# Rotating rope queries from one product instead of two, in a two-layer hybrid backbone on one core

## The chip, the cores and the metric

The kernel runs on 1 core of a Trainium2 chip. The metric is device time of one execution in microseconds (us), as the median of three runs. Within the core, TensorE does matmuls, VectorE and ScalarE read their results from PSUM and write SBUF, GpSimd (POOL in the rows) works on SBUF, and SyncE (SP) issues most of the transfers. Each engine runs its own instructions in order and waits for the others by semaphores.

## The reference, cut to what matters

The reference is a diffusion backbone of two layers over 1024 latent tokens of width 1024, with 256 context tokens. The even layer runs gated linear attention (GLA) and multi-head latent attention (MLA) side by side; the odd layer mixes by Fourier transforms and chunked gating. The change touches one thing, the rope part of the MLA queries. A low-rank latent of 256 is normalised and multiplied by `w_uq`, which gives each of 8 heads 64 plain features and 32 rope features; the rope features are then rotated by an angle for each token, their two halves of 16 acting as the two coordinates:

```python
def apply_rope(x, cos, sin):
    xf = x.astype(jnp.float32)
    x1, x2 = jnp.split(xf, 2, axis=-1)
    return jnp.concatenate([x1 * cos - x2 * sin, x1 * sin + x2 * cos], -1).astype(x.dtype)

q = jnp.einsum('bnr,re->bne', rms_norm(cq, q_norm_g), w_uq).reshape(B, n, MLA_HEADS, MLA_NOPE + MLA_ROPE)
q_nope, q_rope = q[..., :MLA_NOPE], q[..., MLA_NOPE:]
q_rope = apply_rope(q_rope, rope[0][:, None, :], rope[1][:, None, :])
s = (einsum('bqhd,bkhd->bhqk', q_nope, k_nope) + einsum('bqhr,bkr->bhqk', q_rope, k_rope)) * MLA_SCALE
```

Scores, softmax and the product with the values follow for each head over all 1280 keys.

## The kernel before, in words

Everything is held transposed: features on the 128 partitions, tokens along the free dimension in halves of 512. Products are made in three passes (`mm3`, lines 144 to 148): each fp32 operand is split into a high part, rounded to fp32r by ScalarE, and a low part, the difference, by VectorE (`split`, line 131); a product is then high by high, low by high and high by low, accumulated in one PSUM bank. So a contraction over 256 features is six matmuls for 128 output rows and 512 tokens.

The work is written as Python generators that yield an estimate of their cost. `weave` (line 51) advances the stream that has used the smallest share of its weight; the order that results is the program's order, which the framework's own planner then takes as priorities when it lays out each engine's queue. Waits are placed by the framework.

The rope queries are made in `mla_qr` (line 929), four heads at a time: 4 x 32 features are 128 output rows. It is called twice. The first call, for heads 0 to 3, is in `mla_ramp` (line 868). This is the prologue of the attention; it is woven (line 1507) with the last input projections, `in_proj_b`, whose gate tiles need a weight from DRAM, a ScalarE cast and a SiLU. The second call, for heads 4 to 7, is put ahead of the preparation of head 4 and woven with `attend(3)` (lines 1096 to 1104).

A call does for each half of the tokens: load a cosine and a sine table of 128x512 through SP; multiply the latent by the rope columns (one product) and by the same columns with the two halves of each head swapped (a second product, from another 256 columns of the weight); multiply the first by the cosine table, the second by the sine table, whose first 16 rows of each head hold the sine with its sign turned (two VectorE instructions that read PSUM, lines 945 and 946); add them (line 947); and split the sum into `qr`. The weight `k.wq[1]` holds both sets, 512 columns, and is loaded and split at the start of the ramp.

`mla_prep` (line 973) makes one head's operands. Score matmuls contract over 97 partitions: 64 plain features, 32 rope features and one row for the running maximum. These rows have to lie together, so SP moves them from SBUF to SBUF (`move`, line 179): 64 rows of keys (`kt`), 64 plain query rows from `qn` and 32 rope rows from `qr`, each for the high and the low part. All moves are issued by SP in order. Then 24 matmuls `psm` of the high parts give scores for the row maximum, which VectorE reduces; they are the first to use a head's moved rows. `attend` follows, with score matmuls `pss`, exponentials and splits by ScalarE, VectorE and GpSimd, and the value matmuls `psav`. While head h is attended, head h + 1 is prepared.

Of the kernel before, what the change touches and what calls it, by code (L numbers as in the profile page):

```python
# [867 lines left out]
def mla_ramp(k):  # L868

    nc, A = k.nc, k.A  # L870
    k.wq = []
    for i in range(2):
        k.wq.append(k.weight(A["wuq"][i], (P, 2, 512)))
        yield 0.5
    k.cqn = []
    for t in range(2):
        x = k.b4(name="cq")
        nc.sync.dma_start(x, k.cqd[t])
        k.cqn.append(k.split(x, (P, N)))
        yield 0.5  # L880
    x, xc = k.b4(name="ckvr"), k.w2((P, L), name="ckvx")
    nc.sync.dma_start(x, k.ckvd[:, 0:N])
    nc.sync.dma_start(xc, k.ckvd[:, N:])
    cx = k.b4(F32R, (P, 2, L), name="ckx")
    k.ckn = [(a, cx[:, i, :]) for i, a in enumerate(k.split(x, (P, N)))]
    k.split(xc, None, hi=cx[:, 0, :], lo=cx[:, 1, :])
    yield 1.0
    k.wkv = k.weight(A["wukv"], (P, 1024))
    yield 1.0

    k.ktx = k.b4(F32R, (P, 4, L), name="ktx")
    k.kt = [None, None]
    k.Q, k.R = [None] * 8, {}
    yield from mla_qr(k, 0)
    mla_keys(k, 0)
    yield 1.0
    yield from mla_qk(k, 0)
    yield from mla_prep(k, 0)
    assert k.mg_done
    for t in range(4):  # L900
        x = k.b4(name="mg")
        nc.sync.dma_start(x, k.mgd[t])
        k.act(x, x, AF.Silu)
        nc.scalar.dma_start(k.mgd[t], x)
        yield 0.5
# [23 lines left out]
def mla_qr(k, hd):  # L929

    nc, A = k.nc, k.A
    qr = k.R["qr"] = (k.b4(F32R, name="qrh"), k.b4(F32R, name="qrl"))
    for s in range(0, N, 512):
        o = slice(s, s + 512)
        cos, sin = k.w2(name="cos"), k.w2(name="sin")
        nc.sync.dma_start(cos, A["cos"][:, o])
        nc.sync.dma_start(sin, A["sin"][:, o])
        pp = []
        for sw in range(2):
            ps = k.bank()  # L940
            c0 = 256 * sw + 32 * hd
            for kk in range(2):
                k.mm3(ps, (k.wq[1][0][:, kk, c0:c0 + P], k.wq[1][1][:, kk, c0:c0 + P]), (k.cqn[kk][0][:, o], k.cqn[kk][1][:, o]), kk == 0, kk == 1)
            pp.append(ps)
        nc.vector.tensor_tensor(out=cos, in0=pp[0], in1=cos, op=ALU.mult)
        nc.vector.tensor_tensor(out=sin, in0=pp[1], in1=sin, op=ALU.mult)
        nc.vector.tensor_tensor(out=cos, in0=cos, in1=sin, op=ALU.add)
        k.split(cos, None, hi=qr[0][:, o], lo=qr[1][:, o])
        yield 2.6


def mla_qk(k, hd):
# [20 lines left out]
def mla_prep(k, hd):  # L973

    nc = k.nc
    T = nc.tensor
    R = k.R
    if k.kt[hd % 2] is None:
        mla_keys(k, hd % 2)
    q = k.Q[hd] = (k.b4(F32R, (97, 1024), name="qh"), k.b4(F32R, (97, 1024), name="ql"))  # L980
    kt = k.kt[hd % 2]
    r2, r4 = slice(64 * (hd % 2), 64 * (hd % 2) + 64), slice(32 * (hd % 4), 32 * (hd % 4) + 32)
    for i in range(2):
        for c in range(2):
            k.move(kt[i][c][0:64, :], R["kn"][i][c][r2, :])
        k.move(q[i][0:64, :], R["qn"][i][r2, :])
        k.move(q[i][64:96, :], R["qr"][i][r4, :])
    yield 3.0
    mx = k.sm.tile([P, 8, 3], F32, tag="mx", name="mx")
    for i in range(NT):  # L990
        for b, (s, n) in enumerate(KBLK):
            ps = k.bank("psm")
            T.matmul(ps[:, :n], q[0][0:96, i * P:(i + 1) * P], cols(kt[0], s, n)[0:96], start=True, stop=True)  # L993
            nc.vector.reduce_max(out=mx[:, i, b:b + 1], in_=ps[:, :n], axis=AX.X)  # L994
        yield MAXT
    m8 = k.sm.tile([P, 8], F32, tag="m8", name="m8")
    nc.vector.tensor_reduce(out=m8, in_=mx, axis=AX.X, op=ALU.max)
    yield 2.0
    ps = k.bank("psmt")
    T.transpose(ps[0:8, 0:P], m8, k.ident)  # L1000
    mr = k.sm.tile([8, P], F32R, tag="mr", name="mr", bufs=2)
    nc.vector.tensor_copy(out=mr, in_=ps[0:8, 0:P])
    k.move(q[0][96:97, :], mr)
    yield 0.5


def mla(k):
# [81 lines left out]
    for hd in range(8):  # L1089
        st = [(attend(hd), 26.0)]  # L1090
        if hd < 7:
            pre, t = [mla_prep(k, hd + 1)], 5.5 + 8 * MAXT
            if hd % 2 == 0 and hd < 6:
                pre.append(mla_qk(k, hd + 2))
                t += 4.6
            if hd == 3:
                pre.insert(0, scaled(mla_qr(k, 4), 0.8))
                t += 4.2
            st.append((chain(*pre), PREP * t))
        if hd == 6:  # L1100
            st.append((itertools.islice(ahead, EARLY), 2.5 * EARLY))
# [415 lines left out]
def layout(inp):  # L1517
# [45 lines left out]

    mlag = np.concatenate([f("mla_q_norm_g")[0].reshape(2, P), f("mla_kv_norm_g")[0].reshape(1, P)]).T
    uq = f("mla_w_uq")[0].reshape(256, 8, 96)
    un, ur, us = uq[:, :, :64], uq[:, :, 64:], uq[:, :, 64:][:, :, sw]
    uq = np.stack([un.reshape(256, 512), np.concatenate([ur.reshape(256, 256), us.reshape(256, 256)], 1)])
    A["wuq"] = uq.reshape(2, 2, P, 512).transpose(0, 2, 1, 3)
    ukv = f("mla_w_ukv")[0].reshape(P, 8, 128)
    A["wukv"] = np.concatenate([ukv[:, :, :64].reshape(P, 512), ukv[:, :, 64:].reshape(P, 512)], 1)  # L1570
    A["wo0"] = f("even_w_out")[0]
# [37 lines left out]
```

## Time and profile before

| what | value |
|---|---|
| median of three runs | 1150.25 us (1147.44 to 1154.22) |
| the profiled execution's own time | 1148.01 us |
| its span, first to last instruction | 1146.2 us |
| mean granted clock of TensorE | 0.985 of full speed |
| TensorE busy / VectorE busy / ScalarE busy | 1091.3 / 741.2 / 556.9 us |
| `mla_qr`, first call, products | 347.5 to 354.8 us |
| `mla_qr`, second call, products | 524.8 to 531.6 us |

Times in the rows are us from the span's start unless they are marked ns. A timeline row has the start, the duration, the engine, the source line, the operation, output and input tiles, their shape, and in brackets how long the engine was idle before it and what ended that. In a row of windows, each engine's busy us stand with its number of instructions, then TensorE's granted clock (1.00 is full speed), the DMA engines' busy share and the GB/s that they moved. A matmul's recorded duration runs past the start of the next, since matmuls are pipelined.

### The profile page before, as it was taken

To read this page: it belongs to the slowest core of one execution; us is meant where nothing else is said; L and a number is where in the kernel's file an instruction comes from. 1 tells how busy PE (TensorE), PEld (TensorE's weight loads), DVE (VectorE), ACT (ScalarE), POOL (GpSimd) and SP (SyncE) were. 2 spreads that over 40 slices of the span, in tenths; PEclk is the share of its full clock that TensorE was granted. 3 is DMA by queue.
4 is the path that set the end of the run, shared out by engine and by line. 5 is a ranking of instruction groups with operands and counts; after the bars stand their busy time and mean duration, and the time that the engine had idled before them with its cause. 6 is when DMAs were issued, how large, how long until landed. Compare 5 with 4: busy or idle time off the path is not lost.

```text
span 1146.2 us, 14541 instructions
## 1 busy us (share of the span) xinstructions
PE 1091.3 (95%) x5288; PEld 864.7 (75%) x5288; DVE 741.2 (65%) x1256; ACT 556.9 (49%) x956; POOL 255.5 (22%) x252
## 2 busy tenths in 40 slices
PE   5889999899999999999899999999999999999997
PEld 3668778778777777767677666888788888888885
DVE  6867684856655685776677677788526533664544
ACT  6285655576553367867677778313422223332000
POOL 3520000000000023323324366343101000022111
PEclk8989999999999999999999899999999999999999
DMA  9635562333535742213202424323400311125111
GB/s 373 244 129 195 204 225 100 130 119 126 194 121 164 255 131 52 46 25 88 69 3 49 125 74 135 123 110 134 160 1 1 111 37 55 55 71 202 59 55 55
DMA packets 41624, 131.88 MB, mean 115 GB/s; under 512 B 5545, under 2 KB 7337, under 8 KB 41554
## 3 DMA queue, kind: packets, MB, share of 16 engines
q1 hardware_dynamic: 35706, 114.81, 30.6%
q0 software_dynamic: 3056, 10.23, 2.3%
q10 hardware_dynamic: 2792, 5.94, 1.3%
q8 instruction: 41, 0.67, 0.3%
q14 instruction: 29, 0.24, 0.1%
HBM read 98.37 MB, written 20.36 MB: 104 GB/s over the span
## 4 chain that ended last, share of the span: by engine, by line
PE 76%; DVE 7%; ACT 6%; issue 3%; POOL 3%; DMA 3%; SPq 1%; POOLq 0%; DVEq 0%; ACTq 0%
PE ps L146 10%; PE ps L147 10%; PE ps L148 10%; PE pso L148 5%; PE pso L146 5%; PE pso L147 5%; PE pss L1068 3%; PE psm L993 3%; PE pss L1069 3%; PE pss L1070 3%; PE psav L1054 3%; PE psav L1053 3%; PE psav L1052 3%; PE psn L146 1%; PE psn L148 1%
## 5 line engine op out<-in xcount | busy, mean ns | idle before, releaser
L141 POOL TENSOR_TENSOR ph<-pexp,ph 128x512 fp32r<-128x512 f32 x80 | 108.3, 1359 | 175.8 <-ACT ph L136 143.4
L118 ACT ACTIVATE pexp<-pss 128x512 f32<-128x512 f32 x160 | 93.3, 596 | 63.4 <-PE pss L1070 61.7
L146 PE MATMUL ps<-h,hi 128*128 128x512 f32 x256 | 104.0, 418 | 5.6 <-ACT h L328 2.3
L994 DVE TENSOR_REDUCE mx<-psm 128x1 f32<-128x512 f32 (+1 forms) x192 | 102.3, 592 | 10.6 <-PE psm L993 10.4
L148 PE MATMUL ps<-h,lo 128*128 128x512 f32 x256 | 102.9, 402 | 3.1 <-DVE lo L305 1.8
L147 PE MATMUL ps<-h,hi 128*128 128x512 f32 x256 | 104.2, 407 | 0.8 <-DVE h L329 0.8
L141 DVE TENSOR_TENSOR ph<-pexp,ph 128x512 fp32r<-128x512 f32 x80 | 74.8, 940 | 44.4 <-ACT ph L136 42.7
L141 DVE TENSOR_TENSOR lo<-wraw,hi 128x1024 fp32r<-128x1024 f32 x37 | 47.1, 1283 | 85.3 <-ACT hi L136 80.3
L146 PE MATMUL pso<-hi,yh 128*128 128x512 f32 x256 | 99.8, 390 | 0.0
L147 PE MATMUL pso<-lo,yh 128*128 128x512 f32 x256 | 99.7, 390 | 0.0
L148 PE MATMUL pso<-hi,yl 128*128 128x512 f32 x256 | 99.0, 389 | 0.0
L136 ACT CAST ph<-pexp 128x512 fp32r<-128x512 f32 x160 | 95.2, 620 | 2.8
L146 PE MATMUL ps<-h1h,hi 128*128 128x512 f32 x192 | 75.1, 391 | 0.0
L148 PE MATMUL ps<-h1h,lo 128*128 128x512 f32 x192 | 74.7, 389 | 0.0
L147 PE MATMUL ps<-h1l,hi 128*128 128x512 f32 x192 | 74.7, 389 | 0.0
L1135 POOL TENSOR_TENSOR owr<-owr,rowB 128x1024 f32<-128x1024 f32 x16 | 42.4, 2659 | 119.8 <-DMA owr<-wo 119.8
L1054 PE MATMUL psav<-ph,V 128*96 128x512 f32 x160 | 63.8, 399 | 1.4 <-POOL ph L141 1.1
L1052 PE MATMUL psav<-ph,V 128*96 128x512 f32 x160 | 63.3, 396 | 0.2
L146 PEld LDWEIGHTS ps<-h,hi 128*128 128x128 f32 x256 | 48.9, 193 | 18.7 <-ACT h L328 3.9
L148 PEld LDWEIGHTS ps<-h,lo 128*128 128x128 f32 x256 | 49.1, 192 | 17.1 <-DVE lo L305 2.9
L147 PEld LDWEIGHTS ps<-h,hi 128*128 128x128 f32 x256 | 49.6, 194 | 11.5 <-issue 1.4
L148 PEld LDWEIGHTS pso<-hi,yl 128*128 128x128 f32 x256 | 48.0, 188 | 10.1
(358 smaller groups left out, 2590.0 us busy)
## 6 DMA issues: line engine op xcount, KB each, us to landing
aw<-ada SPq DMA_DIRECT2D x32, 512.0 KB, 9.0
araw<-ada SPq DMA_DIRECT2D x32, 512.0 KB, 3.6
wraw<-we SPq DMA_DIRECT2D x16, 512.0 KB, 4.6
owr<-wo SPq DMA_DIRECT2D x16, 512.0 KB, 4.8
xr<-x SPq DMA_DIRECT2D x16, 512.0 KB, 8.6
wraw<-wd SPq DMA_DIRECT2D x12, 512.0 KB, 4.1
xt<-x SPq DMA_DIRECT2D x8, 512.0 KB, 9.9
kt<-kn SPq DMA_DIRECT2D x16, 256.0 KB
```

Of the source, the lines that this page charges most:

```text
L118: r = self.nc.scalar.activation(out=out, in_=in_, func=func, **kw)
L136: self.nc.scalar.copy(out=hi, in_=src)
L141: (lo_eng or self.nc.vector).tensor_tensor(out=lo, in0=src, in1=f32(hi), op=ALU.subtract)
L146: t.matmul(out, lhs[0], rhs[0], start=start, stop=False)
L147: t.matmul(out, lhs[0], rhs[1], start=False, stop=False)
L148: t.matmul(out, lhs[1], rhs[0], start=False, stop=stop)
L993: T.matmul(ps[:, :n], q[0][0:96, i * P:(i + 1) * P], cols(kt[0], s, n)[0:96], start=True, stop=True)
L994: nc.vector.reduce_max(out=mx[:, i, b:b + 1], in_=ps[:, :n], axis=AX.X)
L1052: T.matmul(a[0:96, :], vhi(j, hd), hi, start=j == 0, stop=False)
L1053: T.matmul(a[0:64, :], vlo(j, hd), hi, start=False, stop=False)
L1054: T.matmul(a[0:96, :], vhi(j, hd), lo, start=False, stop=j == NK - 1)
L1135: k.nc.gpsimd.tensor_tensor(out=raw, in0=raw, in1=k.ogate, op=ALU.mult)
```

## The change

The rope weight is loaded with 256 columns, ordered within each group of four heads by half: 64 columns with the first halves of the four heads, then 64 with the second halves. One product of six matmuls then has the first coordinates on partitions 0 to 63 and the second coordinates on 64 to 127. VectorE multiplies it once by the cosine and once by the sine table (now without signs), and combines them across: the first 64 partitions take cosine part minus the sine part of partitions 64 to 127, and the last 64 the cosine part plus the sine part of partitions 0 to 63. A head's 32 rope rows are now two pieces of 16 rows, 64 partitions apart, so `mla_prep` moves each operand's rope rows with two transfers (`rope_move`). The yields and the stage's weight are smaller.

```diff
-    for i in range(2):
-        k.wq.append(k.weight(A["wuq"][i], (P, 2, 512)))
+    for n, w in (("wun", 512), ("wur", 256)):
+        k.wq.append(k.weight(A[n], (P, 2, w)))
         yield 0.5
...
-        nc.sync.dma_start(sin, A["sin"][:, o])
-        pp = []
-        for sw in range(2):
-            ps = k.bank()
-            c0 = 256 * sw + 32 * hd
-            for kk in range(2):
-                k.mm3(ps, (k.wq[1][0][:, kk, c0:c0 + P], k.wq[1][1][:, kk, c0:c0 + P]), (k.cqn[kk][0][:, o], k.cqn[kk][1][:, o]), kk == 0, kk == 1)
-            pp.append(ps)
-        nc.vector.tensor_tensor(out=cos, in0=pp[0], in1=cos, op=ALU.mult)
-        nc.vector.tensor_tensor(out=sin, in0=pp[1], in1=sin, op=ALU.mult)
-        nc.vector.tensor_tensor(out=cos, in0=cos, in1=sin, op=ALU.add)
+        nc.sync.dma_start(sin, A["sinq"][:, o])
+        ps = k.bank()
+        c = slice(32 * hd, 32 * hd + P)
+        for kk in range(2):
+            k.mm3(ps, (k.wq[1][0][:, kk, c], k.wq[1][1][:, kk, c]), (k.cqn[kk][0][:, o], k.cqn[kk][1][:, o]), kk == 0, kk == 1)
+        nc.vector.tensor_tensor(out=cos, in0=ps, in1=cos, op=ALU.mult)
+        nc.vector.tensor_tensor(out=sin, in0=ps, in1=sin, op=ALU.mult)
+        nc.vector.tensor_tensor(out=cos[0:64], in0=cos[0:64], in1=sin[64:128], op=ALU.subtract)
+        nc.vector.tensor_tensor(out=cos[64:128], in0=cos[64:128], in1=sin[0:64], op=ALU.add)
         k.split(cos, None, hi=qr[0][:, o], lo=qr[1][:, o])
-        yield 2.6
+        yield 1.6
+
+
+def rope_move(k, out, x, hd):
+
+    r = 16 * (hd % 4)
+    k.move(out[0:16], x[r:r + 16, :])
+    k.move(out[16:32], x[64 + r:80 + r, :])
...
-        k.move(q[i][64:96, :], R["qr"][i][r4, :])
+        rope_move(k, q[i][64:96, :], R["qr"][i], hd)
...
-                pre.insert(0, scaled(mla_qr(k, 4), 0.8))
-                t += 4.2
+                pre.insert(0, mla_qr(k, 4))
+                t += 3.2
```

The host's layout changes to match: `A["wur"]` holds the reordered rope columns, `A["sinq"]` the sine table without signs.

## Rows read from the trace of the kernel before

**Rows 1.** page, busy time of engines (share, instructions) and the chain's shares

```profile
PE 1091.3 (95%) x5288; PEld 864.7 (75%) x5288; DVE 741.2 (65%) x1256; ACT 556.9 (49%) x956; POOL 255.5 (22%) x252
...
PE 76%; DVE 7%; ACT 6%; issue 3%; POOL 3%; DMA 3%; SPq 1%; POOLq 0%; DVEq 0%; ACTq 0%
```

**Rows 2.** windows of 25 us: busy us of each engine, clock, DMA share, GB/s

```profile
350.00:375.00 25.00, 23.38 (x105) 19.07 (x104) 14.42 (x21) 6.01 (x10) 1.62 (x3) 1.00 0.43 138
...
525.00:550.00 25.00, 25.00 (x112) 18.87 (x111) 18.24 (x32) 15.55 (x28) 7.56 (x6) 1.00 0.28 75
```

**Rows 3.** timeline of TensorE in the ramp: start us, us, line, operation

```profile
352.07 0.39 PE L146 MATMUL ps<-hi 128*128 128x512 f32 x1
...
354.79 0.39 PE L146 MATMUL ps<-h,hi 128*128 128x512 f32 x1
```

**Rows 4.** timeline of TensorE while head 3 attends

```profile
528.91 0.39 PE L146 MATMUL ps<-hi 128*128 128x512 f32 x1
...
531.64 0.40 PE L1068 MATMUL pss<-qh,kt 97*128 97x512 f32 x1
```

**Rows 5.** instructions on tile cos: duration ns min/median/max

```profile
L947 DVE TENSOR_TENSOR cos<-cos,sin x4: 691/692/693, 350.6 to 532.6; 128x512 f32<-128x512 f32 x4
```

**Rows 6.** instructions of line 1061, in the same columns

```profile
L1061 DVE TENSOR_TENSOR rl<-rl,mg x16: 673/689/2833, 445.4 to 716.5; 64x512 f32<-64x512 f32 x16
```

**Rows 7.** timeline of SP: moves of rope rows (head 4), and the ramp's weight

```profile
384.38 1.32 SPq L153 DMA_DIRECT2D wraw<-we  x1
...
534.40 0.56 SPq L181 DMA_DIRECT2D qh<-qrh  x1
```

**Rows 8.** windows of 2 us around waits for moved rows (last: DMA share, GB/s)

```profile
380.00:382.00 2.00, 2.00 (x10) 1.67 (x9) 0.51 (x1) 0.00 (x0) 0.54 (x1) 1.00 0.98 239
...
536.00:538.00 2.00, 2.00 (x11) 1.37 (x10) 0.00 (x0) 1.94 (x5) 0.87 (x1) 1.00 0.93 203
538.00:540.00 2.00, 2.00 (x10) 1.36 (x9) 1.60 (x3) 1.40 (x3) 0.53 (x1) 1.00 0.03 8
...
568.00:570.00 2.00, 0.00 (x0) 0.00 (x0) 0.66 (x1) 0.00 (x0) 0.11 (x1) 1.00 1.01 232
...
572.00:574.00 2.00, 2.00 (x11) 1.64 (x10) 2.00 (x4) 1.53 (x3) 0.33 (x1) 1.00 0.00 0
```

**Rows 9.** timeline of TensorE where it stopped, and head 4's first use

```profile
362.01 0.50 PE L146 MATMUL ps<-h,hi 128*128 128x512 f32 x1 [1.62 <-ACT hi L136]
...
383.72 0.70 PE L993 MATMUL psm<-kt,qh 96*128 96x512 f32 x2 [0.64 <-DMA qh<-qrh]
...
490.33 0.70 PE L993 MATMUL psm<-kt,qh 96*128 96x512 f32 x2 [1.39 <-DMA qh<-qrh]
...
539.77 0.63 PE L993 MATMUL psm<-kt,qh 96*128 96x512 f32 x2
...
570.79 0.70 PE L993 MATMUL psm<-kt,qh 96*128 96x512 f32 x2 [3.11 <-DMA qh<-qrh]
...
651.79 0.80 PE L1068 MATMUL pss<-qh,ktx 97*128 97x512 f32 x1 [1.62 <-DVE mx L994]
```

**Rows 10.** timeline of VectorE in the ramp

```profile
349.32 0.69 DVE L945 TENSOR_TENSOR cos<-ps,cos 128x512 f32<-128x512 f32 x1 [1.92 <-PE ps L148]
349.93 0.68 DVE L946 TENSOR_TENSOR sin<-ps,sin 128x512 f32<-128x512 f32 x1
```

**Rows 11.** instructions of line 181 (moves), duration ns min/median/max

```profile
L181 SPq DMA_DIRECT2D qh<-qrh x8: 558/586/1068, 379.6 to 637.9; - x8
```

**Rows 12.** timeline of ScalarE in the ramp

```profile
360.43 0.60 ACT L118 ACTIVATE gg<-ps 128x512 f32<-128x512 f32 x1 [6.62 <-PE ps L148]
360.92 1.04 ACT L136 CAST hi<-wraw 128x1024 fp32r<-128x1024 f32 x1
```

**Rows 13.** windows of 4 us around the stop at 651 (clock third from last)

```profile
652.00:656.00 4.00, 4.00 (x10) 3.14 (x11) 3.83 (x7) 2.50 (x4) 0.26 (x1) 0.50 0.02 4
656.00:660.00 4.00, 4.00 (x15) 2.93 (x14) 4.00 (x5) 4.00 (x9) 4.00 (x3) 0.73 0.00 0
```

More of the change, by code (lines that the diff above doesn't have):

```diff
@@ L981, in mla_prep @@
     kt = k.kt[hd % 2]
-    r2, r4 = slice(64 * (hd % 2), 64 * (hd % 2) + 64), slice(32 * (hd % 4), 32 * (hd % 4) + 32)
+    r2 = slice(64 * (hd % 2), 64 * (hd % 2) + 64)
     for i in range(2):
@@ L1565, in layout @@
     uq = f("mla_w_uq")[0].reshape(256, 8, 96)
-    un, ur, us = uq[:, :, :64], uq[:, :, 64:], uq[:, :, 64:][:, :, sw]
-    uq = np.stack([un.reshape(256, 512), np.concatenate([ur.reshape(256, 256), us.reshape(256, 256)], 1)])
-    A["wuq"] = uq.reshape(2, 2, P, 512).transpose(0, 2, 1, 3)
+    un, ur = uq[:, :, :64].reshape(2, P, 512), uq[:, :, 64:].reshape(2, P, 2, 4, 2, 16)
+    A["wun"] = un.transpose(1, 0, 2)
+    A["wur"] = ur.transpose(1, 0, 2, 4, 3, 5).reshape(P, 2, 256)
+    A["sinq"] = np.tile(si, (8, 1)).astype(np.float32)
     ukv = f("mla_w_ukv")[0].reshape(P, 8, 128)
```

## The prediction

> **What bounds the kernel now.** I read the page first: its busy table and its chain of waits. TensorE is busy for 1091.3 of 1146.2 us and holds 76% of the chain that ended last, VectorE 7%, ScalarE 6% [rows 1]. An average hides stages, so next come the windows of 25 us around the two places where the rope queries are made: the ramp (heads 0 to 3, about 345 to 364 us) and the stage in which head 3 attends while head 4 is prepared (about 510 to 550 us). TensorE is busy 23.38 and 25.00 of 25 us there, VectorE 14.42 and 18.24, ScalarE 6.01 and 15.55 [rows 2]. So TensorE's own work sets the pace at both, and a product taken out should bring the stage's end forward unless something else becomes late. The third view is TensorE's timeline, for the price of a product and for the few stops between products.
>
> **What it removes.** A half (512 tokens) of the rope rotation has two products of 2 x 3 matmuls now; it will have one, so 6 matmuls go. There are two halves in a call and two calls: 24 matmuls go, of 48. The price is not the 0.39 us recorded for one: in the ramp the twelve matmuls of the second half start at 352.07 and the next work starts at 354.79, 2.72 us for 12, or 0.227 us each [rows 3]. In head 3 the twelve that start at 528.91 give way at 531.64, 2.73 us [rows 4]. So a product is 1.36 us, and four of them 5.45 us.
>
> Two readings of the same rows differ here. The recorded durations would give 24 x 0.39 = 9.4 us. The Trainium skill, Perfetto Trace Analysis (Identifying the Most-Contended Engine), calls matmul busy time a bad measure because matmuls are pipelined; by that rule the starts decide and the gain is 5.45 us. The starts are what I sum.
>
> A small part that goes too: the rope weight is 256 columns and not 512, so half of one cast and one subtraction of 128x1024 and 256 KB of load. They sit on ScalarE, VectorE and SP ahead of the ramp's rope, under TensorE's projection matmuls; nothing on the path, 0.
>
> **What it adds on VectorE.** A half has two multiplications, one addition and one subtraction now. The addition becomes two of 64 partitions whose second operand lies 64 partitions away. No row shows such an operands' offset. Nearest rows: the present addition of 128x512 takes 0.692 us [rows 5], and an operation of 64x512 with both inputs in SBUF takes 0.673 to 2.833 us, median 0.689 [rows 6]; fewer partitions are not faster. I take 0.69 (the median, and the fastest is close to it), the bounds are 0.67 and 2.83. Against one addition of 0.69 that is +0.69 a half and 2.8 us over four, bounds 2.6 and 19.9. It cannot be a gain, since one instruction becomes two. VectorE has 7 to 10 us free in each 25 there [rows 2], so it costs TensorE nothing, unless the rotated rows come late for head 4. There the move of the rotated rows is issued at 534.40 [rows 7], all transfers have ended by 538 (the DMA share falls from 0.93 to 0.03) [rows 8], and TensorE first uses them at 539.77 [rows 9]: at least 1.8 us of slack. Afterwards TensorE arrives 2.72 us sooner; the rows arrive 2.72 sooner less 0.69 for the extra operation and 0.59 to 1.17 for one or two extra moves, so the slack ends between 0.5 us and about zero. I take 0; the upper bound, with a slow operation of 2.83 and both extra moves, is 2.2 us.
>
> Back to back, VectorE's multiplications start 0.61 us apart although each is recorded at 0.69 [rows 10]: neighbours overlap by 0.08 us. The Trainium skill, VectorE: DVE Perf Modes (Two Vector instructions with no wait between them), speaks against the new pair: an instruction whose inputs start in another group of 32 partitions than the last ones did is held until all earlier ones have finished. By it the two combinations and the operation after them lose the overlap, 3 x 0.08 us a half; the sum by it stays the same, but head 4's rows lose another 0.24 to 0.48 us.
>
> **What it adds on SP and the DMA rings.** Each head's rope rows are moved by four transfers of 16 rows, not two of 32: two more issues a head, 16 in all, with the same bytes. A move of rope rows takes SP 0.558 to 1.068 us, median 0.586 [rows 11]. SP is not the bound, but TensorE does wait for these moves: 0.64 us at 383.72 (head 0, in the ramp), 1.39 at 490.33 (head 3), 3.11 at 570.79 (head 5) [rows 9]. Behind the moves, in order on SP, stands in the ramp the last gate weight, issued at 384.38 [rows 7], which the last projection tile waits for; later, the moves of the same head's low parts. I price four places: these three and head 7, which is prepared in the same turn of the loop as heads 3 and 5. One extra issue ahead of the last rows of qh costs TensorE between 0 and 1.07 us at each. Around the waits the DMA engines are busy for 0.98 and 1.01 of the time [rows 8], so bytes and not issues set the landing; I stay near zero, 0.15 us each: +0.6 us, bounds 0 and 4.3. A 16-row transfer that ran worse than a 32-row one is not shown by any row; it is inside that bound.
>
> **Order.** The program's order comes from shares of weighted streams and a planner behind them, and the weights change (2.6 to 1.6 a half; 4.2 to 3.2 for the stage). Later work of the ramp is issued some two or three groups of six matmuls earlier against the projections. That moves no work but can move stops. Two are known: at 362.01 TensorE idles 1.62 us because a weight's cast stands behind a SiLU on ScalarE, and at 651.79 it idles 1.62 us for VectorE [rows 9, 12]. After the second the granted clock is 0.50 and 0.73 for two stretches of 4 us (the lower level of 1.2 GHz part of the time) [rows 13], 2.0 + 1.1 = 3.1 us lost; after the longer stop at 570.79 it stays at 1.00 [rows 8]. So a stop costs 1.6 us, or 4.7 with the clock.
>
> **Sum.** -5.45 + 0.6 = -4.85 us. The profiled execution took 1148.01 us (span 1146.2 and 1.8 around it), so 1143.2; it was 2.2 us below the median of the three runs, and on the median's scale the forecast is 1150.25 - 4.85 = 1145.4 us, 0.42% less.
>
> **Rivals.**
> 1. A stop goes as the order shifts: the one at 362 (-1.6: 1143.8 us) or the one at 651 with its clock (-4.7: 1140.7 us). For it: both come from instruction order, not from work. Against: the stage around 651 is far behind the change and merely shifts. Chance 0.24.
> 2. A stop of the second kind is added, most likely in the ramp, where casts queue behind SiLUs: -4.85 + 4.7 = -0.15, 1150.1 us. For it: ScalarE's order gave just this stop already. Against: the ramp gets emptier. Chance 0.19.
> 3. Slower than before: the rope moves. All four waits grow by the slow issue of 1.07 us (4.3) and the clock falls after one of them (3.1) or two (6.2): +1.9 us, 1152.2, or +5.0, 1155.3. It decides once added waiting and lost clock pass 5.45 us together, so not without the clock. For it: waits of 1.39 and 3.11 us on exactly these rows stand there now. Against: the rings are full then, and the clock held through 3.11 us. Chance 0.10.
> 4. It doesn't take the TensorE time out, since another engine ends last in both stages: about 1150.2 us. Against it stand 25.00 of 25 us. Chance 0.02.
> The forecast has the remaining 0.45, with its own range 1143.5 to 1147.5.
>
> **How the numbers follow.** 0.5% is 5.75 us, about what a measurement of this kernel can tell from no change: below 1144.5 is faster, above 1156.0 slower. Faster: nearly all of rival 1 (0.22) and the lower end of the forecast (0.14): 0.36. Slower: the far half of rival 3 and what lies beyond it, 0.08. The rest, 0.56, is within. The range runs from 1140.0 (rival 1 with the clock) to 1152.5 (rival 3 with one fall of the clock); it leaves out part of rivals 1 and 3 and the far ends of the unknown costs, some 0.15.
>
> **What would show it.** TensorE's instructions fall by 24 matmuls; each half shows six starts in 1.36 us, followed at once by other work. The pair of combinations shows 0.67 to 0.75 us each. The moves are 32 of rope rows with 0.5 to 0.6 us of issue, and TensorE's waits for them stay 5 to 6 us in total. From the attention's start on the whole trace is about 2.5 us early, from head 5 on about 5. Wrong would be: waits for rope rows above 8 us in total, an operation of the pair well over 1 us, rows of head 4 waited for, or a new stretch below full clock between 345 and 725 us.

## The result and the profile after

The changed kernel takes 1163.8 us (median of 5 runs, 1160.93 to 1167.71); the kernel before, beside it, 1151.71 us (1147.44 to 1154.22). The ratio is 1.0112 with a 95% interval of 1.0077 to 1.0146: about 13 us slower, where 0.4% faster was forecast. The profiled execution took 1167.71 us, the slowest of the five, so its stages show 4 us more than the median; the one before, 1148.01 us, lies 3.7 us below its own. So the two profiles differ by 19.7 us where the medians differ by 12.

The page of the changed kernel, to be read against [rows 1]: 24 matmuls fewer as foretold, TensorE's busy time longer all the same, and its share of the chain lower.

```profile
PE 1094.5 (94%) x5264; PEld 863.7 (74%) x5264; DVE 746.8 (64%) x1260; ACT 556.9 (48%) x956; POOL 255.8 (22%) x252
...
PE 74%; DVE 8%; ACT 6%; issue 5%; POOL 3%; DMA 3%; SPq 1%; POOLq 0%; DVEq 0%; ACTq 0%
```

Its windows of 25 us in the ramp, in head 3's attention and in the last head (columns as in [rows 2]). TensorE was 23.38 and 25.00 busy in the first and third of these before; now the ramp's next window has 16.42 at a clock of 0.80, head 3's 24.35, and the last head's 22.70.

```profile
350.00:375.00 25.00, 24.73 (x111) 20.16 (x110) 18.89 (x26) 9.27 (x15) 1.62 (x3) 1.00 0.54 177
375.00:400.00 25.00, 16.42 (x62) 13.03 (x61) 11.49 (x20) 5.10 (x7) 1.08 (x2) 0.80 0.71 184
525.00:550.00 25.00, 24.35 (x106) 17.78 (x105) 17.82 (x23) 19.38 (x36) 8.30 (x6) 1.00 0.37 95
...
686.00:711.00 25.00, 22.70 (x95) 15.77 (x94) 14.79 (x12) 20.50 (x38) 15.16 (x9) 1.00 0.26 85
```

TensorE's waits (in total us, times, longest) in the changed kernel. The first row was 5.1 us in all in the kernel before, worked out from the stops of [rows 9].

```profile
PE psm L998 <- DMA qh<-qrh: 9.5, 2, 8.6
...
PE psm L998 <- DMA ql<-qnl: 3.7, 2, 3.0
...
PE psav L1059 <- POOL ph L141: 3.2, 5, 0.8
...
PE psav L1059 <- DVE ph L141: 2.3, 2, 1.2
```

To see where the time lies, I cut both traces at landmarks: the first matmul of the rope product (`ps<-hi`), the first score matmul `pss`, the fourth, sixth and eighth move of a maximum row (`qh<-mr`, issued by SP when a head's row maxima are done), and the first matmul of the output projection (`pso<-hi,yh`). The landmarks of the changed kernel are 349.74, 424.54, 522.49, 604.40, 685.46 and 726.82; those of the kernel before 345.27, 413.90, 510.27, 590.73, 669.78 and 707.19. Lengths between them in us, one profiled execution each; the other kernels are those of the experiments:

| stage | before | after | e1 | e4 | e13 | e5 | e9 | e14 |
|---|---|---|---|---|---|---|---|---|
| A: ramp, to the first `pss` | 68.63 | 74.80 | 68.95 | 68.96 | 73.71 | 65.59 | 67.18 | 65.61 |
| B: heads 0 to 2 | 96.37 | 97.95 | 99.11 | 99.80 | 97.81 | 97.03 | 97.48 | 97.50 |
| C: heads 3, 4 (second call) | 80.46 | 81.91 | 79.08 | 80.03 | 79.18 | 84.46 | 82.22 | 80.66 |
| D: heads 5, 6 | 79.05 | 81.06 | 79.16 | 80.97 | 80.25 | 79.42 | 79.26 | 78.93 |
| E: last head | 37.41 | 41.36 | 41.34 | 41.33 | 37.42 | 37.43 | 37.44 | 37.43 |
| sum | 361.92 | 377.08 | 367.64 | 371.09 | 368.37 | 363.93 | 363.58 | 360.13 |

The five stages account for 15.2 of the 19.7 us between the two spans. The other 4.5 us came before any changed product ran (345.27 against 349.74). I give them no cause in the change: in the sixteen profiles of this study the first rope product starts anywhere from 344.6 to 350.9 us.

Of the 15.2 us, 6.2 are in the ramp, and the reading there is short. TensorE's timeline has its last projection matmul at 377.69 and nothing until 386.66; before, it had matmuls until 382.70 and then the stop of 0.64 in [rows 9].

```profile
377.69 0.39 PE L148 MATMUL ps<-h,lo 128*128 128x512 f32 x1
386.66 1.19 PE L998 MATMUL psm<-kt,qh 96*128 96x512 f32 x2 [8.58 <-DMA qh<-qrh]
```

The name in the brackets is the last move to land, not the cause. ScalarE's timeline of the same moment shows why the moves are issued no earlier: the casts of the keys, `kn`, stand behind a gate's SiLU and a weight's cast, and ScalarE sat idle 3.98 us for that gate's product.

```profile
378.12 0.60 ACT L118 ACTIVATE gg<-ps 128x512 f32<-128x512 f32 x1 [3.98 <-PE ps L148]
378.61 1.04 ACT L136 CAST hi<-wraw 128x1024 fp32r<-128x1024 f32 x1
379.54 1.08 ACT L136 CAST kn<-ps 128x512 fp32r<-128x512 f32 x2
```

In the kernel before, ScalarE's order is the other way round: weight first, then queries and keys, then the gate.

```profile
375.20 1.05 ACT L136 CAST hi<-wraw 128x1024 fp32r<-128x1024 f32 x1
376.15 1.08 ACT L136 CAST qnh<-ps 128x512 fp32r<-128x512 f32 x2
377.11 1.09 ACT L136 CAST kn<-ps 128x512 fp32r<-128x512 f32 x2
378.06 0.65 ACT L118 ACTIVATE gg<-ps 128x512 f32<-128x512 f32 x1
```

So SP can issue the key rows, and the plain and rope rows behind them in its order, only from 380.65 on (the rope pairs take 1.85 and 2.73 us of issue), and no projection stands ahead of the first `psm` in TensorE's queue to cover that.

```profile
380.65 0.49 SPq L181 DMA_DIRECT2D kt<-kn  x1
381.19 0.59 SPq L181 DMA_DIRECT2D qh<-qnh  x1
381.83 1.85 SPq L181 DMA_DIRECT2D qh<-qrh  x2
...
385.44 2.73 SPq L181 DMA_DIRECT2D ql<-qrl  x2
```

The order on ScalarE does not make the stop by itself. Counted from the first rope matmul, `kn` is cast at 29.80 us here and at 29.93 us in e1, the experiment below, which has no such stop. What differs is TensorE's own order: between the first rope matmul and the first `psm` stand 160 matmuls before, 124 in the changed kernel and 148 in e1 (windows of the three, in this order; TensorE is the second column). Twelve of the 36 that are missing are the first call's two products that went; the other 24, four groups of six, stand behind the `psm` now. At 0.227 us each they are 5.4 us of the stop; the rest is time that the kernel before and e1 lose ahead of the `psm`, above all in a stop for a weight's cast, 1.62 us before and 1.92 in e1; here that stop is 0.27.

```profile
345.27:383.71 38.44, 36.20 (x160) 29.39 (x159) 20.96 (x29) 12.44 (x20) 2.16 (x4) 1.00 0.50 155
349.74:386.65 36.91, 28.07 (x124) 22.63 (x123) 22.49 (x31) 12.04 (x19) 2.16 (x4) 0.95 0.58 180
348.87:386.51 37.64, 35.20 (x148) 28.40 (x147) 22.48 (x31) 12.07 (x19) 2.16 (x4) 0.95 0.56 168
```

The stop costs more than itself: in windows of 2 us the granted clock falls to 0.50, the lower level of 1.2 GHz, and stays there for some 6 us after TensorE is at work again.

```profile
380.00:382.00 2.00, 0.00 (x0) 0.00 (x0) 2.00 (x3) 0.62 (x2) 0.00 (x0) 1.00 0.13 31
382.00:384.00 2.00, 0.00 (x0) 0.00 (x0) 0.70 (x2) 0.00 (x0) 0.54 (x1) 0.67 0.99 201
...
388.00:390.00 2.00, 2.00 (x7) 1.52 (x6) 1.08 (x3) 0.00 (x0) 0.00 (x0) 0.50 0.72 115
...
392.00:394.00 2.00, 2.00 (x9) 1.57 (x8) 0.62 (x2) 1.05 (x1) 0.00 (x0) 0.77 1.03 217
```

Stage E is the second place: no changed product is anywhere near, and it is 3.9 us longer. Three theories came from this. **O**: the smaller yields alone make the new order and its stop. **M**: the added transfers cost by themselves. **T**, formed after e1 to e4: added moves cost because the planner lays the other engines out differently around them, not because they are transfers.

### The profile page after: what moved, and what is told of

Same layout as the page of the kernel before. It is cut to its first block, busy times and chain, and to the rows that moved or that the text cites. A ratio compares the mean times of both kernels' runs of the same rounds, so it can differ in the third digit from the quotient of the medians.

```text
span 1165.9 us, 14522 instructions
## 1 busy us (share of the span) xinstructions
PE 1094.5 (94%) x5264; PEld 863.7 (74%) x5264; DVE 746.8 (64%) x1260; ACT 556.9 (48%) x956; POOL 255.8 (22%) x252
## 4 chain that ended last, share of the span: by engine, by line
PE 74%; DVE 8%; ACT 6%; issue 5%; POOL 3%; DMA 3%; SPq 1%; POOLq 0%; DVEq 0%; ACTq 0%
PE ps L146 11%; PE ps L147 11%; PE ps L148 11%; PE pso L146 5%; PE pso L148 5%; PE pso L147 5%; PE psm L998 3%; PE pss L1073 2%; PE pss L1074 2%; PE pss L1075 2%; PE psav L1059 2%; PE psav L1058 2%; PE psav L1057 2%; POOL ph L141 1%; PE psn L146 1%
## 5 line engine op out<-in xcount | busy, mean ns | idle before, releaser
L146 PE MATMUL ps<-h,hi 128*128 128x512 f32 x256 | 105.2, 423 | 4.2 <-ACT h L328 2.3
L147 PE MATMUL ps<-h,hi 128*128 128x512 f32 x256 | 105.7, 413 | 0.8 <-DVE h L329 0.8
L141 DVE TENSOR_TENSOR lo<-wraw,hi 128x1024 fp32r<-128x1024 f32 (+1 forms) x37 | 46.6, 1267 | 85.3 <-ACT hi L136 80.2
L998 PE MATMUL psm<-kt,qh 96*128 96x512 f32 x128 | 44.9, 417 | 15.5 <-DMA qh<-qrh 9.5
```

The costliest lines, as they stand in the source:

```text
L141: (lo_eng or self.nc.vector).tensor_tensor(out=lo, in0=src, in1=f32(hi), op=ALU.subtract)
L146: t.matmul(out, lhs[0], rhs[0], start=start, stop=False)
L147: t.matmul(out, lhs[0], rhs[1], start=False, stop=False)
```

## Experiments

Each was timed beside the kernel before; a ratio is against that, with its 95% interval. One per mille is 1.15 us. Code and profile rows left out are marked by `...`.

**e1, the ramp's yield put back.**

```diff
-        yield 1.6
+        yield 2.6 if hd == 0 else 1.6
```

> The changed kernel with one number put back: the first call of mla_qr (in the ramp) yields 2.6 again for each half instead of 1.6, so the planner weighs the ramp against the input projections as before. No work differs from the changed kernel. Theory O (order): the smaller yield let ScalarE's casts of the keys (kn) fall behind a gate SiLU and a weight's cast, and TensorE's 8.6 us stop at 378 us with the slow clock behind it comes from that; then this kernel loses the stop and is 9 to 13 us faster than the changed one, 1149 to 1154 us, with the wait for qh<-qrh in the ramp under 2 us. Theory M (moves): the stop is the price of the rope rows moved in 16 transfers more; then the wait stays near 8 us and the time near 1162 to 1166 us.

Measured: 1157.42 us, ratio 1.0042 [1.0026, 1.0058], 0.7% below the changed kernel by the two ratios. The stop of 8.58 us is gone: the projection runs up to 386.29, and the first `psm` follows without a wait. Stage A is 68.95. The time is above theory O's 1149 to 1154 and below theory M's 1162. What stays is not theory O's: stage E is still 41.34.

```profile
386.29 0.39 PE L148 MATMUL ps<-h,lo 128*128 128x512 f32 x1
386.52 0.63 PE L998 MATMUL psm<-kt,qh 96*128 96x512 f32 x2
```

**e2, one move of 32 rows.**

```diff
-    k.move(out[0:16], x[r:r + 16, :])
-    k.move(out[16:32], x[64 + r:80 + r, :])
+    k.move(out, x[2 * r:2 * r + 32, :])
```

> The changed kernel with each head's rope rows moved by one transfer of 32 neighbouring rows for each operand, as before (the rows are then partly those of another head; everything else as changed). Theory O: the ramp's stop stays at 6 to 9 us and the time at 1158 to 1164 us; at most 2 us come back from the shorter queue on SP. Theory M: the wait falls under 2 us and the time to 1147 to 1153 us.

Measured: 1156.99 us, 1.0033 [1.0015, 1.0051]. The ramp's stop stays (7.56 us at 383.60), as theory O has it; stage E is back at 37.43, and the time lies between the two theories'.

**e3, the new yields and stage weight in the kernel before.**

```diff
-        yield 2.6
+        yield 1.6
...
-                pre.insert(0, scaled(mla_qr(k, 4), 0.8))
-                t += 4.2
+                pre.insert(0, mla_qr(k, 4))
+                t += 3.2
```

> The kernel before with nothing changed but the numbers that steer the order: mla_qr yields 1.6, the stage of head 3 gets 3.2 for it and is not scaled. Two products, three VectorE operations and two moves stay. Theory O: the same stop appears with all the old work, 7 to 10 us of waiting at the ramp's first psm, and the time is 7 to 13 us over the kernel before, 1158 to 1165 us. Theory M: no change, 1149 to 1154 us.

Measured: 1158.64 us, 1.0053 [1.0031, 1.0075]. With both products still there the stop of the ramp appears, 7.59 us at 386.79. So it is made by numbers that compute nothing: 136 matmuls stand ahead of the first `psm` here, 24 fewer than before, as in the changed kernel.

**e4, the moves cut in two in the kernel before.**

```diff
-        k.move(q[i][64:96, :], R["qr"][i][r4, :])
+        for z in range(2):
+            k.move(q[i][64 + 16 * z:80 + 16 * z, :], R["qr"][i][r4.start + 16 * z:r4.start + 16 * z + 16, :])
```

> The kernel before with each 32-row move of rope rows cut into two of 16 rows, nothing else. Theory O: 0 to 3 us slower than before, 1151 to 1155 us, with the waits for qh<-qrh at 5 to 8 us in total. Theory M: 6 to 12 us slower, 1157 to 1164 us.

Measured: 1160.67 us, 1.0066 [1.0040, 1.0092]: some 8 us for 16 more transfers of the same bytes. Neither theory alone holds: order and moves each cost 6 to 8 us. But TensorE's waits for `qh<-qrh` are only 6.3 us in all here, 1.2 more than before. Of the 9.2 us that the five stages of its profile are longer than before, 3.9 lie in the last head, where no rope row is waited for; 3.4 lie in heads 0 to 2, where TensorE waits 1.84 us for rope rows at 419.42 and the clock falls behind that. The stops of the last head add up to 4.2 us, as in the changed kernel, against 1.1 before; one of them in TensorE's timelines (the first fence is the changed kernel, the second e4):

```profile
707.10 0.48 PE L1059 MATMUL psav<-ph,V 128*96 128x512 f32 x1 [1.07 <-DVE ph L141]
```

```profile
697.30 0.48 PE L1055 MATMUL psav<-ph,V 128*96 128x512 f32 x1 [1.08 <-DVE ph L141]
```

The instructions of TensorE, ScalarE and VectorE are the same as before in number; their order is not. Before, VectorE's split of `ph` (686.28) stood ahead of the scaling `rl` (687.56); in e4 it stands behind it (the first fence is VectorE's timeline of the kernel before, the second that of e4):

```profile
686.28 1.36 DVE L141 TENSOR_TENSOR ph<-pexp,ph 128x512 fp32r<-128x512 f32 x1 [0.56 <-ACT ph L136]
687.56 1.78 DVE L1061 TENSOR_TENSOR rl<-rl,mg 64x512 f32<-64x512 f32 x1
```

```profile
693.78 1.78 DVE L1062 TENSOR_TENSOR rl<-rl,mg 64x512 f32<-64x512 f32 x1
695.49 1.76 DVE L141 TENSOR_TENSOR ph<-pexp,ph 128x512 fp32r<-128x512 f32 x1
```

That is theory T, and the next two runs test it.

**e7, the moves cut in two, the second piece issued by GpSimd** (kernel before).

```diff
-        k.move(q[i][64:96, :], R["qr"][i][r4, :])
+        k.move(q[i][64:80, :], R["qr"][i][r4.start:r4.start + 16, :])
+        nc.gpsimd.dma_start(f32(q[i][80:96, :]), f32(R["qr"][i][r4.start + 16:r4.start + 32, :]))
```

> The kernel before with each 32-row rope move cut in two 16-row moves, as in e4, but the second piece issued by GpSimd. The instruction order of TensorE, ScalarE and VectorE is then that of before; SP issues as many moves as before. Theory T (the order that the planner makes of two more SP moves is what cost 8.3 us in e4): as before, 1152, within 1.5 us. Theory H (16-row transfers cost by themselves, in landing or on the rings): 5 to 8 us slower, 1157 to 1160, with waits of TensorE for qrh above 6 us.

Measured: 1150.89 us, 1.0003 [0.9984, 1.0023]. Sixteen-row pieces cost nothing that can be measured when the other engines keep their order; stage E is 37.44. Of theory H its waits alone came: the stops for rope rows add up to 7.9 us (those for `ql` included), and the time is unchanged.

**e13, the same edit in the changed kernel.**

```diff
-    k.move(out[16:32], x[64 + r:80 + r, :])
+    k.nc.gpsimd.dma_start(f32(out[16:32]), f32(x[64 + r:80 + r, :]))
```

> The changed kernel with one edit: of each pair of rope moves the second is issued by GpSimd and not by SP. The transfers and their bytes are those of the changed kernel. Theory T (the cost of the moves is the order that the planner makes of two more SP moves): the stops on ph in the last head go, the ramp's stop of 7.5 to 8.6 us stays, and the time is as in e2, 1156 to 1158. Theory H (16-row transfers cost by themselves): as the changed kernel, 1162 to 1165.

Measured: 1157.08 us, 1.0047 [1.0031, 1.0063], as theory T has it. Stage E goes from 41.36 to 37.42 with all transfers in place; the ramp's stop stays:

```profile
383.09 1.19 PE L998 MATMUL psm<-kt,qh 96*128 96x512 f32 x2 [7.85 <-DMA qh<-qrh]
```

**e8, sixteen transfers of 64 bytes that nothing waits for** (kernel before).

```diff
+    if hd == 0:
+        k.tr = k.spill("tr", 16, 16)
...
         k.move(q[i][64:96, :], R["qr"][i][r4, :])
+        nc.sync.dma_start(k.tr[2 * hd + i:2 * hd + i + 1, :], f32(R["qr"][i][r4.start:r4.start + 1, 0:16]))
```

> The kernel before with 16 more transfers on SP, one behind each rope move, of 64 bytes to DRAM that nothing waits for; TensorE's and VectorE's order is that of before. Theory S (one more SP issue of 0.59 us ahead of the next moves is the price): two issues a head, 2 to 5 us slower, with later ql and kt rows. Theory T (order): nothing, 1152, within 1.5 us.

Measured: 1152.79 us, 1.0014 [0.9991, 1.0037], which is -1 to +4 us. It leaves a small price of SP's issues open. It also narrows theory T: SP has as many more instructions as in e4, and yet stage E is 37.42 and TensorE's matmuls come in the order of before. So it is not their number alone that changes the plan; these have nothing waiting for them, the rope moves have. Whether that is what counts was not tested.

**e5, one product and the pair, with yields, weight and number of moves as before.** In the changed kernel, and with rows partly of other heads as in e2:

```diff
-        yield 1.6
+        yield 2.6
...
-    k.move(out[0:16], x[r:r + 16, :])
-    k.move(out[16:32], x[64 + r:80 + r, :])
+    k.move(out, x[2 * r:2 * r + 32, :])
...
-                pre.insert(0, mla_qr(k, 4))
-                t += 3.2
+                pre.insert(0, scaled(mla_qr(k, 4), 0.8))
+                t += 4.2
```

> The changed kernel with the yields and the stage's weight of before, and each head's rope rows moved by one transfer of 32 rows (rows partly of other heads, so the scores differ; the work is the same). What is left of the change: 24 matmuls fewer and the pair on VectorE. Theory A (order, moves and products add up; from the four runs so far order +6.3, moves +8.3, sum +11.5): products alone about -3.1 us against before, 1149 beside 1152. Theory P (the step of the prediction holds in full): -5.45 us, 1147. Theory N (the time taken out is lost to the next stop whatever the moves are): 0, 1152.

Measured: 1152.67 us, 1.0015 [0.9995, 1.0035]. Theory N: -5.45 and -3.1 lie outside the interval, which is -0.6 to +4.0 us. The stages say where. A is 3.04 shorter than before, as promised; C is 4.00 longer where 2.73 less was promised, with a clock of 0.94 over it against 1.00. In C, TensorE stops for `ph` of head 3, right behind the second call, where it had run through without a stop before:

```profile
537.74 0.47 PE L1058 MATMUL psav<-ph,V 128*96 128x512 f32 x1 [0.28 <-POOL ph L141]
539.23 0.47 PE L1056 MATMUL psav<-ph,V 128*96 128x512 f32 x1 [1.02 <-ACT ph L136]
541.93 0.74 PE L1058 MATMUL psav<-ph,V 128*96 128x512 f32 x1 [1.99 <-DVE ph L141]
```

ScalarE's timeline shows what holds `ph`: the rounding of the rotated rows waits 1.01 us for the pair's second operation, and head 3's cast stands behind it.

```profile
532.86 1.30 ACT L118 ACTIVATE pexp<-pss 128x512 f32<-128x512 f32 x2
535.17 0.62 ACT L136 CAST qrh<-cos 128x512 fp32r<-128x512 f32 x1 [1.01 <-DVE cos L945]
535.70 0.61 ACT L136 CAST ph<-pexp 128x512 fp32r<-128x512 f32 x1
```

VectorE's shows why that operation was late: the first of the pair took 1.69 us, not 0.69, while GpSimd ran a split from 532.52 to 533.89.

```profile
532.75 1.69 DVE L944 TENSOR_TENSOR cos<-cos,sin 64x512 f32<-64x512 f32 x1
534.45 0.68 DVE L945 TENSOR_TENSOR cos<-cos,sin 64x512 f32<-64x512 f32 x1
```

And the clock falls after it, as windows of 4 us of e5 show (clock third from last):

```profile
540.00:544.00 4.00, 2.07 (x6) 1.65 (x7) 2.31 (x3) 0.00 (x0) 1.33 (x1) 0.52 0.00 0
544.00:548.00 4.00, 4.00 (x14) 3.26 (x14) 3.04 (x6) 1.69 (x3) 0.00 (x0) 0.63 0.00 0
```

**e6, one move with a step of four partitions.** The columns are ordered by half, feature and head, so a head's 32 rows are every fourth partition; yields and weight as before.

```diff
-    k.move(out[0:16], x[r:r + 16, :])
-    k.move(out[16:32], x[64 + r:80 + r, :])
+    k.move(out, x[hd % 4:P:4, :])
...
-    A["wur"] = ur.transpose(1, 0, 2, 4, 3, 5).reshape(P, 2, 256)
+    A["wur"] = ur.transpose(1, 0, 2, 4, 5, 3).reshape(P, 2, 256)
...
```

> The weight's columns are ordered by half, then by feature, then by head, so that a head's 32 rope rows are every fourth partition, and one transfer with a step of four partitions moves them in order; yields and weight of before. The full computation. If the number of transfers is what costs (and what it does to the order): as e5, 1147 to 1149, faster than before. If the scattered rows themselves cost (theory M, landing): the waits psm<-qrh grow as in the changed kernel and it is 4 us or more above e5.

Measured: 1153.77 us, 1.0024 [1.0004, 1.0045], as e5 within the intervals: the step costs nothing that shows, and the second call's loss is here too. The next kernels build on it.

**e9, one product for heads 0 to 3 only.** e6, with 384 columns of the weight: heads 4 to 7 have two products, one addition and the signed table again.

```diff
-    for n, w in (("wun", 512), ("wur", 256)):
+    for n, w in (("wun", 512), ("wur", 384)):
...
-        ps = k.bank()
-        c = slice(32 * hd, 32 * hd + P)
+        pp = []
+        for c0 in ((128, 256) if hd else (0,)):
+            ps = k.bank()
+            c = slice(c0, c0 + P)
...
```

> Heads 0 to 3 rotated from one product (columns by half, feature, head; one move with a step of four partitions), heads 4 to 7 as before from two products; yields and weight of before. The order of TensorE, ScalarE and VectorE behind the ramp is then that of before. The full computation. Theory V (the second call's gain is lost in head 3's attention, the first call's 2.7 to 3.0 us is real): about -3 us, 1149 beside 1152, TensorE at 25.00 of 25 us in 525:550 with the clock at 1.00. Theory N (any gain in the ramp is lost to later stops): 1152.

Measured: 1151.10 us, 0.9996 [0.9977, 1.0014]. In C, TensorE is again 25.00 of 25 us busy at 1.00 from 525 to 550, as theory V says, but the time is not 3 us less. C is 82.22 even so, 1.8 us longer than before with the same products: TensorE stops 3.70 us for head 5's low rows, and the clock falls behind that. The first call's 3.0 us are there in stage A wherever the clock held from 350 to 375 us (e5, e14: A is 65.6), and half of it is gone where the clock was 0.93 there (e9: 67.18).

**e10, e5 without the pair.**

```diff
-        nc.vector.tensor_tensor(out=cos[0:64], in0=cos[0:64], in1=sin[64:128], op=ALU.subtract)
-        nc.vector.tensor_tensor(out=cos[64:128], in0=cos[64:128], in1=sin[0:64], op=ALU.add)
+        nc.vector.tensor_tensor(out=cos, in0=cos, in1=sin, op=ALU.add)
```

> e5 without the pair: the two tables' products are added by one VectorE instruction of 128x512, as before (so neither the signs nor the rows are those of the rotation). Theory V (in the second call the pair makes the rotated rows late, ScalarE waits for them with head 3's casts behind, and TensorE runs out of ph): the stops of 3.3 us at 537 to 542 shrink below 1.5 us, the clock in 525:550 stays at 1.00, and the time is 3 to 5 us below e5, 1148 to 1150. Theory B (TensorE has 1.36 us less of other work in each half, so ph is late with or without the pair): stops of 2.5 us or more stay, time as e5, 1152 to 1153.

Measured: 1149.87 us, 0.9985 [0.9966, 1.0004]. Between the theories: against e5 the clock from 525 to 550 stays 1.00 and the time is 3.5 us less (0.3 to 6.6), so the pair counts; but 1.88 us of stops stay without it. That they were 3.29 in e5 is not shown to be the pair's doing, since the six other kernels with it, and with its rounding on ScalarE, have 1.42 to 2.18. Nor is the slow operation: the single addition took 1.77 us here, at 531.91.

```profile
537.78 0.48 PE L1055 MATMUL psav<-ph,V 128*96 128x512 f32 x1 [1.23 <-ACT ph L136]
539.13 0.47 PE L1057 MATMUL psav<-ph,V 128*96 128x512 f32 x1 [0.65 <-POOL ph L141]
```

**e11, e6 with the second call's rounding on GpSimd.**

```diff
-        k.split(cos, None, hi=qr[0][:, o], lo=qr[1][:, o])
+        k.split(cos, None, hi=qr[0][:, o], lo=qr[1][:, o], hi_eng="pool" if hd else "act")
```

> e6 with the rounding of the second call's rotated rows on GpSimd and not on ScalarE, so that no wait for them stands ahead of head 3's casts. The full computation. Theory V: the stops at 540 to 546 shrink below 1.5 us and the time falls by 2 to 4 us against e6, to 1150 to 1152. Theory B: stops stay, 1153 to 1154; GpSimd's own splits of ph, behind a rounding of 1.3 us, may make it worse, 1155.

Measured: 1148.74 us, 0.9981 [0.9959, 1.0002]. The time is below what theory V gave, but not as V had it: a stop of 2.29 us stays. C is 78.76 against e5's 84.46, with 1.5 us less of stops in all; most of the difference is the clock, at 1.00 here over the stage and at 0.94 there.

**e12, e6 with the changed kernel's weight for head 3's stage** and the ramp's yield of before.

```diff
-        yield 2.6
+        yield 2.6 if hd == 0 else 1.6
...
-                pre.insert(0, scaled(mla_qr(k, 4), 0.8))
-                t += 4.2
+                pre.insert(0, mla_qr(k, 4))
+                t += 3.2
```

> e6 with the changed kernel's yield and weight in the stage of head 3 (1.6 and 3.2), and the ramp's yield of before. The full computation. If the place of the second call's products in head 3's attention matters: stops there of 1.9 us as in e2, with the clock at 1.00, so 2 to 4 us below e6, 1150 to 1152. If not: as e6, 1153 to 1154.

Measured: 1149.82 us, 0.9990 [0.9972, 1.0008], 3.9 us below e6, as the first reading has it. The stops behind the second call add up to 2.18 us. This is the changed kernel without its two order costs: what the products and the pair are worth is -1.2 us, -3.2 to +0.9.

**e14, e11 and e12 together.** Both diffs, on e6.

```diff
-        k.split(cos, None, hi=qr[0][:, o], lo=qr[1][:, o])
-        yield 2.6
+        k.split(cos, None, hi=qr[0][:, o], lo=qr[1][:, o], hi_eng="pool" if hd else "act")
+        yield 2.6 if hd == 0 else 1.6
...
```

> e11 with the changed kernel's yield and weight in the stage of head 3 (e12's edit). The full computation. If the remaining stop of 2.3 us in head 3's attention comes from where the second call's products stand: it falls below 1.5 us and the time is 1 to 2 us below e11, about 1147. If it comes from TensorE having 1.36 us less of other work in each half: a stop of about 2 us stays and the time is as e11, 1148 to 1149.5.

Measured: 1148.44 us, 0.9966 [0.9945, 0.9988]. A stop of 2.07 us stays, so it comes from the work that is missing and not from where the products stand in head 3.

```profile
540.17 0.48 PE L1057 MATMUL psav<-ph,V 128*96 128x512 f32 x1 [2.07 <-DVE ph L141]
```

This version beats both kernels: 0.34% below the one before, and 1.4% below the changed one by the two ratios.

## Why the prediction was wrong, step by step

Three steps failed. The changed order was priced at nothing, the two moves instead of one at 0.6 us, and each cost 7 to 8 us; and the second call's gain was taken in full.

**Products: count and price right, the gain half wrong.** 24 matmuls went, and starts stay 0.227 us apart. The first call gave what was promised where the clock held: A falls by 3.04 us in e5, of which 2.73 are the twelve matmuls; in the profiles where it fell behind the ramp's stop of 1.92 us (1.62 before), as in e9, about half is left. The second call's 2.73 us came in part at best; C rose by 4.00 in e5 and by 1.45 in the changed kernel. C is no clean measure of it, though: with all the old products it is 82.22 in e9, 82.99 in e8 and 84.01 in e3, where the clock fell behind the stop for head 5's rows. In the four profiles with one product and a clock of 1.00 over the stage (e1, e10, e11, e13), C is 78.76 to 79.44, 1.0 to 1.7 shorter than before. The step that failed is the reading of 25.00 busy of 25 us [rows 2] as "a product taken out should bring the stage's end forward". It says that TensorE did not wait; it does not say by how much it did not. The twelve matmuls of each half's two products were also the time in which ScalarE, VectorE and GpSimd made `ph`. With six, TensorE comes to the value matmuls too early: it stops for `ph` behind the second call for 1.42 to 3.29 us in all ten kernels with one product there, and not at all in five of the six with two. The sixth, e4, stops 1.70 us at 546.07, so another order alone can make such a stop too. The fourth rival, an engine that ends last in the stage, had the mechanism for the second call and was given 0.02.

**The pair: size right, cover wrong.** The pair was 0.69 us an operation in the median, as taken, and 1.68 us once in stage C, inside the bound of 2.83; that one is no price of the pair, since the single addition took 1.77 at the same place in e10 (instructions on the tile `cos`, duration in ns min/median/max, for the first of the pair):

```profile
L944 DVE TENSOR_TENSOR cos<-cos,sin x4: 687/688/1682, 354.2 to 544.7; 64x512 f32<-64x512 f32 x4
```

Its starts are 0.70 us apart in the ramp where other neighbours start 0.61 apart, as VectorE's timeline of the changed kernel shows. The Trainium skill, VectorE: DVE Perf Modes (Two Vector instructions with no wait between them), holds an instruction whose inputs start in another group of 32 partitions than the last ones did until all earlier ones have finished. The trace agrees with it. Two such gaps a half are new, not three: the addition of the kernel before already started 0.72 us behind the multiplication ahead of it (349.93 to 350.65).

```profile
352.88 0.69 DVE L942 TENSOR_TENSOR cos<-ps,cos 128x512 f32<-128x512 f32 x1 [1.01 <-PE ps L148]
353.49 0.68 DVE L943 TENSOR_TENSOR sin<-ps,sin 128x512 f32<-128x512 f32 x1
354.21 0.69 DVE L944 TENSOR_TENSOR cos<-cos,sin 64x512 f32<-64x512 f32 x1
354.91 0.69 DVE L945 TENSOR_TENSOR cos<-cos,sin 64x512 f32<-64x512 f32 x1
355.62 0.69 DVE L942 TENSOR_TENSOR cos<-ps,cos 128x512 f32<-128x512 f32 x1
```

What the prediction missed is who waits. It looked for the rotated rows of head 4, and had slack there. But their rounding stands in ScalarE's queue ahead of head 3's casts, so whatever makes the rows late delays head 3, at once (1.01 us in e5).

**Moves: 0.6 us, bounds 0 and 4.3; it was 7.5 us, 3 to 12** (the changed kernel against e13, by the ratios; 8 in e4). The step that failed is the term itself, worked out for the wrong thing: waits for the moved rows. As transfers the pieces cost nothing that shows (e7, -1.8 to +2.6 us), which is near the value taken; SP's issues were 0.59 us in the median, as taken. The price is the order that the planner makes when SP has these moves, too. The part of it that is shown is 3.9 us in E, far from any wait for rope rows: E is 41.33 to 41.36 in the three kernels with the pieces on SP and 37.41 to 37.46 in the thirteen others. The rest has no such fixed place: against before, B is 1.6 to 3.4 longer in the three and D 0.1 to 2.0, with falls of the clock among them. Rival 3 had the sign, and the wrong mechanism: it needed waits of 4.3 us and a lost clock.

**Order: nothing in the sum, and 4.7 us in rival 2; it was 8 us, 4 to 12** (the changed kernel against e1; 6 in e3). The step that failed is "that moves no work but can move stops", sized by the stops that stood there already. The prediction had the cause in hand: the ramp's later work comes "some two or three groups of six matmuls earlier against the projections". It was four groups, 24 matmuls, and at 1.36 us a group they were 5.4 us of cover for the moves of head 0. Rival 2 named the place, the ramp, and sized the cost by a stop of 1.62 us behind a cast; the stop was 8.58 us. Casts behind SiLUs are there, but counted from the first rope matmul those of the keys come no later than in e1, which has no such stop. And it was one of two order costs, which it had no room for.

**Sum by parts.** What is left when both order costs are taken out is -1.2 us (e12); 7.5 and 8 us on top give 14, beside the 13 that were measured. The parts fit within their intervals, but not closely: from e12's side, e1 puts the moves at 6 and e2 the ramp's yield at 5. How the planner comes from two more moves to another order in the last head was not traced, and stays open.

Of the signs that were to show it wrong, three came: waits for rope rows above 8 us (9.5), an operation of the pair well over 1 us (1.68) and a new stretch below full clock between 345 and 725 us (382 to 394).

## What to carry to other kernels

Where a planner lays out the queues, an edit's cost estimates and its added instructions are part of the change: compare the order on every engine before and after, and keep the old numbers until the arithmetic alone has been measured. When an engine stops, count first what it still had ahead of that place in the other kernel; the transfer that landed last may have been no later. An engine that is busy all the time has slack towards its suppliers that the profile does not print; before taking work off it, see how early its inputs were ready at that place. A transfer that costs time on one queue may be free on another, as e4 and e7 show.

## What the runs showed that was not expected

- The clock's falls decide as much as the stops, and one profile shows only one throw of them. The same 1820 matmuls brought the first rope product at 344.6 us in one profile (e10) and at 350.9 in another (e6); in the changed kernel the window 250 to 275 had a clock of 0.86, before 1.00, with TensorE 22.75 and 22.76 us busy in them. A stop of 3.29 us in several pieces (e5) was followed by a clock of 0.52; one of 2.29 (e11) was not, nor were the 3.11 us of [rows 9]. So the length of a stop did not decide it here.
- VectorE's operations of 0.69 us took 1.68 to 1.78 us while GpSimd ran a split, where both of their inputs lie in SBUF. One that reads PSUM kept its time: in the changed kernel `mg<-psav,rl` took 0.68 us at 551.94, inside a split that ran from 551.71 to 552.98. GpSimd itself rounds 128x512 in 0.63 us, as long as ScalarE takes (0.62), where its split takes 1.27 (its timeline in e11):

```profile
535.82 0.63 POOL L138 TENSOR_SCALAR qrh<-cos 128x512 fp32r<-128x512 f32 x1 [2.06 <-DVE cos L945]
536.40 1.27 POOL L141 TENSOR_TENSOR ph<-pexp,ph 128x512 fp32r<-128x512 f32 x1
```
